# Larger groups of exact dots, the order of the last gathers and fewer address checks in a hard-max attention kernel

## The chip, the core and the metric

The kernel runs on one core of one Trainium2 chip. Its time is device microseconds of one execution; several executions are timed and their median is taken. Engine names: PE is TensorE, DVE is VectorE, ACT is ScalarE, POOL is GpSimd, SP is SyncE.

## What is computed

```python
B, Sq, Sk, D = 4, 4096, 4096, 128          # q, k, v in float32
logits = q @ k.transpose(0, 2, 1)
best = argmax(logits, axis=-1)
out = v[b, best, :]
```

For each of 16384 query rows the key with the largest dot product is found, and the value row of the same index is the result. No softmax is taken.

## The kernel before

**Tiles.** The 16384 queries are 128 tiles of 128 rows (`T = 128`), 32 tiles to a batch (`NQT = 32`). Keys come in groups of four. TensorE forms fp16 sums and differences of keys, so that the maximum of a group can be had from few products; ScalarE (`A`, `E`) and VectorE (`W`) evict them. `W` holds, for each query and each of 1024 groups, a score in the upper half of a word and the group's code in the lower half. `MAX8` (L264) takes the eight largest words of a row, so the best group comes with its score.

**Which of the four keys.** For the best group the kernel gathers one row of fp16 differences per query from a scratch copy of the keys (`k16`, 768 bytes) with an indirect DMA on GpSimd (L282, tile `kg`, "key gather" below). VectorE multiplies it with the query (`dots`: `prod` L300, `p1` L305, `p2` L308, reduction to `D` L310) and picks the largest of four (`pick`, L320 to L333). The result `win` is the index of the value row. It is gathered by an indirect DMA on GpSimd (L341, tile `vr`, "value gather" below) and stored by SP (L346).

**Chunks.** `cuts` (L682) divides the tiles into chunks: twelve of eight tiles up to tile 96, seven of four up to 124, one of two, and the last two tiles on a path of their own (`gather_whole`, `dots_whole`, `pick_whole`, in fp32). A pick treats one chunk. A dot treats `m` tiles: four where the chunk ends at tile 72 or before (`T - 56`), two after that (L776).

**The order of the work** is written out by hand: the tile framework keeps the order of the program on every engine. Iteration `it` (0 to 127) issues the products of tile `it`, the fold L260 of tile `it - 1`, the maximum L264 of tile `it - 2`, and twice a `step`, which lets the running dots, picks and flag work go on by an instruction or so. A four-tile dot yields `("wait", 1)`, one iteration, between most of its instructions; a two-tile dot goes on at the next step. Then `gathers(it - 2)` makes the candidates (L276) when a group of `m` tiles is complete and puts its key gathers into `near_q`; `issue(it)` (L743) takes from the queues what GpSimd issues in this iteration:

- from `near_q` one key gather, or two when more than `behind`'s limit are queued;
- from `fast` one gather for flagged rows, at most every second iteration;
- from `late_q` up to two value gathers, as `room` allows. `room` grows by `rate` an iteration (2.42, 2.5, 2.55, 3.0 by the iteration's number) and falls by one for each gather issued. A value tile's store follows two iterations later through SP.

GpSimd runs its gathers in this order, each one after the one before.

**The end.** Queries whose best two scores lie close together are flagged and computed again in fp32. The first 64 tiles' flags are treated inside the loop (`flag_segment`), the last 64 by `flags_last` after it: it gathers the listed queries and three candidate groups each (L512, tiles `FQ` and `FK`, "group gathers" below), computes exact dots (`exact`, L594), gathers the value rows (`FV`, L512 again) and scatters them to the output (L541). Before the group gathers it issues `LATE = 6` value gathers, after them the rest of `late_q`. Value gathers and the gathers of `flags_last` have an address check (`bounds_check`): an index beyond the table is skipped without error. Key gathers have none.

Of the kernel before, what the change touches and what calls it, by code (L numbers as in the profile page):

```python
# [17 lines left out]
IOA = bass.IndirectOffsetOnAxis  # L18
# [3 lines left out]
TAU = 8.0  # L22
NEAR = 0.5
SLOTS = 6
LATE = 6
NKG = 6


# [1 line left out]
def kernel(ctx, tc, q, k, v, out):  # L30
    nc = tc.nc
    B, Sq, D = q.shape
    Sk = k.shape[1]
    P = 128
    NQT = Sq // P
    T = B * NQT
# [229 lines left out]
    fast, near_q, late_q = [], [], []  # L266
    kg_t, cand_t = {}, {}
    done, stores, marks = set(), set(), set()
    wait_q = []

    def gather(c, t0, n):
        c0, c1 = chunks[c]
        if t0 == c0:
            cand_t[c] = sp.tile([P, c1 - c0], U32, tag=f"cand{c1 - c0}", name=f"cand_{c}", bufs=6)
        x = cand_t[c][:, t0 - c0:t0 - c0 + n]
        nc.vector.tensor_scalar(out=x, in0=TOP.bitcast(U32)[:, t0:t0 + n, 0], scalar1=IDX, scalar2=IDX,  # L276
                                op0=OP.bitwise_and, op1=OP.bitwise_xor)
        kg = rp.tile([P, 4, 3, P], FP16, tag="kg", name=f"kg_{t0}", bufs=NKG)[:, 0:n]
        assert len(kg_t) < NKG
        kg_t[t0] = kg  # L280
        for j in range(n):
            near_q.append(lambda j=j: nc.gpsimd.indirect_dma_start(  # L282
                out=kg[:, j].rearrange("p f d -> p (f d)"), out_offset=None, in_=k16[t0 // NQT],
                in_offset=IOA(ap=x[:, j:j + 1], axis=0)))
        mark = lambda: done.add(("kg", t0))
        marks.add(mark)
        near_q.append(mark)
        start(dots(c, t0, n), "dots", c)
# [24 lines left out]
    def pick(c, t0, t1):  # L313
        n = t1 - t0
        b, qt = t0 // NQT, t0 % NQT
        d = D_t[c % 4][:, 0:n, :]
        yield "until", lambda: all(("dot", x) in done for x in range(t0, t1)), 0
        cand = cand_t.pop(c)
        mx = sp.tile([P, n, 1], FP32, tag=f"mx{n}", name=f"mx_{c}")
        nc.vector.tensor_reduce(out=mx[:, :, 0], in_=d, axis=AX_X, op=OP.max)  # L320
        yield "dve",
        near = sp.tile([P, n, 4], FP32, tag=f"near{n}", name=f"near_{c}")
        nc.vector.scalar_tensor_tensor(out=near, in0=d, scalar=NEAR, in1=mx.to_broadcast([P, n, 4]),
                                       op0=OP.add, op1=OP.is_ge)
        yield "dve",
        sel = sp.tile([P, n, 4], FP32, tag=f"sel{n}", name=f"sel_{c}")
        nc.vector.tensor_tensor(out=sel, in0=near, in1=iota8.unsqueeze(1).to_broadcast([P, n, 4]), op=OP.mult)
        yield "dve",
        nc.vector.tensor_reduce(out=CNT[:, t0:t1], in_=sel, axis=AX_X, op=OP.add)
        done.add(("cnt", c))  # L330
        yield "cnt",
        win = sp.tile([P, n], U32, tag=f"win{n}", name=f"win_{c}")
        nc.vector.scalar_tensor_tensor(out=win, in0=CNT[:, t0:t1], scalar=float(b * Sk - 8), in1=cand, op0=OP.add, op1=OP.add)  # L333
        for i in range(0, n, 4):
            put_values(c, i, n, win, out[b].rearrange("(p t) d -> p t d", p=P)[:, qt + i:qt + min(i + 4, n)])

    def put_values(c, i, n, win, dst):
        vr = rp.tile([P, 4, P], FP32, tag="vr", name=f"vr_{c}_{i}", bufs=10)
        m = min(4, n - i)
        for j in range(m):  # L340
            late_q.append(lambda j=j: nc.gpsimd.indirect_dma_start(out=vr[:, j, :], out_offset=None, in_=v_flat,  # L341
                                                                   in_offset=IOA(ap=win[:, i + j:i + j + 1], axis=0),
                                                                   bounds_check=B * Sk - 1, oob_is_err=False))

        def store():
            nc.sync.dma_start(out=dst, in_=vr[:, 0:m])  # L346
            if i + m == n:
                done.add(("out", c))

        stores.add(store)  # L350
        late_q.append(store)

    def put_rec(t0, t1):
        nc.sync.dma_start(out=rec.rearrange("(p t) w -> p t w", t=T)[:, t0:t1, :], in_=TOP.bitcast(U32)[:, t0:t1, :])
# [111 lines left out]
    def flags_last(t0, t1, ready, fill, late):  # L466
# [44 lines left out]
        def get(dst, src, idx, hi):  # L511
            nc.gpsimd.indirect_dma_start(out=dst, out_offset=None, in_=src, in_offset=IOA(ap=idx, axis=0),  # L512
                                         bounds_check=hi - 1, oob_is_err=False)

        late(LATE)
        get(FK[:, 0, :], k_flat, gb[:, 0:1], B * Sk)
# [39 lines left out]
    def gather_whole(t):  # L556
        i = t - (T - 2)
        if i == 0:
            X_t["c"] = sp.tile([P, 2], U32, tag="xc", name="xc", bufs=1)
        c = X_t["c"][:, i:i + 1]  # L560
        nc.vector.tensor_scalar(out=c, in0=TOP.bitcast(U32)[:, t:t + 1, 0], scalar1=IDX, scalar2=IDX | (B - 1) * Sk,
                                op0=OP.bitwise_and, op1=OP.bitwise_xor)
        kk = X_t[i] = fp.tile([P, 512], FP32, tag=f"xk{i}", name=f"xk{i}")
        near_q.append(lambda: nc.gpsimd.indirect_dma_start(out=kk, out_offset=None, in_=k_flat, in_offset=IOA(ap=c, axis=0)))
# [114 lines left out]
    dpart(0, 1)  # L679
    nc.vector.tensor_copy(out=iota_h, in_=iota_r)  # L680
    nc.vector.tensor_copy(out=rec2[:, :, 1], in_=iota_p.to_broadcast([P, SLOTS]))
    cuts = list(range(0, T - 32 + 1, 8)) + list(range(T - 28, T - 3, 4)) + [T - 2, T]  # L682
    chunks = list(zip(cuts[:-1], cuts[1:]))
    SEGS = [0, T // 2, T]
    live = []
# [1 line left out]
    def start(g, kind, c=None):  # L687
        live.append({"g": g, "kind": kind, "c": c, "wake": 0, "until": None, "n": 0})
# [40 lines left out]
    def take_late(n):  # L729
        while n > 0 and late_q:  # L730
            g = late_q.pop(0)
            n -= g not in stores
            g()
        while late_q and late_q[0] in stores:
            wait_q.append((clock[0] + 2, late_q.pop(0)))
# [3 lines left out]
    def put_out(now):  # L739
        while wait_q and wait_q[0][0] <= now:  # L740
            wait_q.pop(0)[1]()

    def issue(it):  # L743
        n = 0
        clock[0] = it
        put_out(it)
        behind = len([g for g in near_q if g not in marks]) > (2 if it >= TAIL else 4)
        while near_q and (n < 1 + behind or near_q[0] in marks):
            g = near_q.pop(0)
            n += g not in marks  # L750
            g()
        if fast and it >= rest[0]:
            fast.pop(0)()
            rest[0] = it + 2
            n += 1
        if it < 16:
            take_late(2 if n == 0 and len(late_q) > 4 else 1)
            return
        b, qt = it // NQT, it % NQT
        busy = 0.7 if qt % 2 == 0 and (10 <= qt < 18 and b + 1 < B or 18 <= qt < 26 and b + 2 < B) else 0.0  # L760
        if qt in (13, 17) and b + 1 < B:
            busy += 1.0
        rate = 2.42 if it < 72 else 2.5 if it < 104 else 2.55 if it < 120 else 3.0
        room[0] = min(room[0] + rate - busy, 3.0) - n
        for i in range(2):
            if room[0] >= 1 and late_q:
                take_late(1)
                room[0] -= 1

    room = [0.0]  # L770

    def gathers(t):
        if t >= T - 2:
            gather_whole(t)
        for c, (t0, t1) in enumerate(chunks):
            m = 4 if t1 <= T - 56 else 2  # L776
            if t0 <= t < t1 and t < T - 2 and (t - t0) % m == m - 1:
                gather(c, t - m + 1, m)
            if t == t0 and t < T - 2:
                start(pick(c, t0, t1), "pick", c)  # L780
        if t % 8 == 7:
            put_rec(t - 7, t + 1)
        if t == SEGS[1] - 1:
            last = [c for c, x in enumerate(chunks) if x[1] == t + 1][0]
            start(flag_segment(0, t + 1, lambda: ("cnt", last) in done, lambda: ("out", last) in done), "flags")
# [6 lines left out]
    for it in range(T):  # L792
# [35 lines left out]
        if it >= 2:  # L828
            gathers(it - 2)
        issue(it)  # L830

    def flush():
# [21 lines left out]
    screen(T)  # L854
    top(T - 2)
    gathers(T - 2)
    flush()
    fold(T - 1)
    late_now(1)
    top(T - 1)  # L860
    gathers(T - 1)
    flush()
    assert not left("flags") and not fast
# [42 lines left out]
```

## Time and profile before

| | |
|---|---|
| Median of 6 runs | 531.04 us (525.3 to 534.13) |
| Profiled execution, its own time | 519.81 us |
| Its span, first to last instruction | 517.9 us |
| Mean granted TensorE clock | 0.905 |
| Value gathers (L341), `vr<-in_v_dram,win` | 126, mean 1040 ns |
| Key gathers (L282) | 126, mean 986 ns |
| Products of the dots (L300), two tiles each | 63, mean 549 ns |
| Fold (L260) and maximum (L264) | 128 each, mean 1303 and 1222 ns |
| Start of the last fold, of the last maximum | 480.30, 481.63 us |
| End of the span | 517.9 us |

The profile is of one execution, which was shorter than each of the six timed runs. Times inside it are microseconds from the span's start. Start-to-start distances can be shorter than durations, since the next instruction of an engine may start before the one before has ended. "Issue" as the reason of a wait means that the profile shows nothing the engine waited for.

### The profile page before, as it was taken

How to read it: one execution, taken by the hardware profiler on the slowest of the kernel's cores; microseconds unless marked ns; L12 is line 12 of the kernel's file. 1: busy time of each engine (PE TensorE's matmuls, PEld its weight loads, DVE VectorE, ACT ScalarE, POOL GpSimd, SP SyncE). 2: the span in 40 equal slices, each digit the busy share in tenths (PEclk: the TensorE clock that was granted, in tenths of full speed). 3: DMA queues.
4: the chain of work that ended last, by engine and by line, in shares of the span. 5: the costliest groups of instructions: out<-in, count | busy, mean ns of one | idle time of the engine just before them, and what ended most of it. 6: DMA issues, size and time to landing. Idle time of an engine off the chain costs nothing.

```text
span 517.9 us, 6303 instructions
## 1 busy us (share of the span) xinstructions
PE 401.6 (78%) x1830; PEld 172.5 (33%) x1830; DVE 411.2 (79%) x770; ACT 381.4 (74%) x437; POOL 309.1 (60%) x335
## 2 busy tenths in 40 slices
PE   8999999979859997879788873849875976978010
PEld 4444444424314442334334331313331322333000
DVE  3688999969949997679959992957995866979842
ACT  3999999969849996789778863848874965977000
POOL 9244557765745777456746774463775673654771
PEclk9999999989979999899979996987997996999555
DMA  7936895622266996222438831441223131222341
GB/s 139 209 58 110 147 125 130 110 76 80 73 132 99 157 157 128 65 72 68 114 83 145 146 91 36 88 116 51 78 72 89 44 105 46 71 73 66 83 135 38
DMA packets 52869, 50.55 MB, mean 98 GB/s; under 512 B 34136, under 2 KB 40890, under 8 KB 52832
## 3 DMA queue, kind: packets, MB, share of 16 engines
q0 software_dynamic: 19072, 33.87, 33.9%
q1 hardware_dynamic: 33760, 16.26, 13.1%
q8 instruction: 14, 0.23, 0.2%
q14 instruction: 23, 0.19, 0.1%
HBM read 40.05 MB, written 14.55 MB: 105 GB/s over the span
## 4 chain that ended last, share of the span: by engine, by line
PE 28%; issue 26%; ACT 23%; POOL 10%; DVE 6%; DMA 4%; another core or an unknown queue 2%; POOLq 0%; ACTq 0%; DVEq 0%
ACT A L234 18%; PE psn L225 9%; PE pd L225 9%; PE psn L244 9%; POOL vr L341 5%; ACT E L247 4%; POOL kg L282 4%; DMA vr<-in_v_dram,win 2%; DVE TOP L264 2%; DVE W L260 2%; DMA natk<-in_k_dram 1%; PE uk L202 1%; DMA kg<-k,cand 1%; PE uk L201 0%
## 5 line engine op out<-in xcount | busy, mean ns | idle before, releaser
L234 ACT ACTIVATE A<-pd 128x1024 f16<-128x1024 f32 x256 | 260.4, 1039 | 43.8 <-PE pd L225 21.4
L260 DVE SCALAR_TENSOR_TENSOR W<-psn,E 128x1024 int16<-128x1024 f32 x128 | 166.7, 1303 | 77.8 <-PE psn L244 36.9
L282 POOL DMA_INDIRECT kg<-k,cand x126 | 124.2, 986 | 141.7 <-DVE cand L276 107.7
L225 PE MATMUL pd<-kT,qT 128*128 128x512 f16 x512 | 158.9, 393 | 38.1 <-issue 19.7
L225 PE MATMUL psn<-kT,qT 128*128 128x512 f16 x512 | 158.7, 392 | 32.2 <-ACT A L234 13.6
L225 PEld LDWEIGHTS <-qT 128*128 128x128 f16 x1024 | 100.6, 100 | 215.0 <-issue 133.0
L341 POOL DMA_INDIRECT vr<-in_v_dram,win x126 | 131.0, 1040 | 50.0 <-issue 37.0
L244 PE MATMUL psn<-A,identh 128*128 128x512 f16 x512 | 159.0, 393 | 0.0
L264 DVE MAX8 TOP<-W 128x8 f32<-128x1024 f32 x128 | 156.4, 1222 | 0.0
L247 ACT ACTIVATE E<-psn 128x1024 int16<-128x1024 f32 x128 | 132.0, 1031 | 21.5 <-PE psn L244 14.1
L244 PEld LDWEIGHTS <-identh 128*128 128x128 f16 x512 | 51.2, 100 | 65.7 <-issue 8.5
L300 DVE TENSOR_TENSOR prod<-kg,natq 128x768 f16<-128x768 f16 x63 | 34.6, 549 | 2.4 <-DMA kg<-k,cand 1.5
L205 ACT ACTIVATE kT<-uk 128x256 f16<-128x256 f32 x48 | 19.8, 413 | 22.5 <-remote 13.9
L201 PE MATMUL uk<-identh,natk 128*128 128x128 f16 x96 | 15.8, 218 | 6.0 <-ACT E L247 5.7
L305 DVE TENSOR_TENSOR p<-prod 128x384 f16<-128x384 f16 (+1 forms) x45 | 19.3, 430 | 0.1
L310 DVE TENSOR_REDUCE D<-p 128x6 f32<-128x192 f16 (+1 forms) x45 | 18.7, 418 | 0.1
L202 PEld LDWEIGHTS <-natk 128*128 128x128 f16 x96 | 9.3, 97 | 13.4 <-issue 10.8
L308 DVE TENSOR_TENSOR p<-p 128x192 f16<-128x192 f16 (+1 forms) x45 | 13.0, 290 | 0.1
L66 POOL DMA_DIRECT2D natk<-in_k_dram x19 | 11.3, 601 | 0.8 <-POOLq L890 0.8
L201 PEld LDWEIGHTS <-natk 128*128 128x128 f16 x96 | 9.4, 98 | 5.6
L484 PE MATMUL fp_e<-n_e,tri 128*128 128x1 f32 x2 | 0.6, 362 | 13.2 <-DVE e_e L478 13.2
L69 POOL DMA_DIRECT2D natq<-in_q_dram x15 | 9.1, 611 | 0.0
(152 smaller groups left out, 141.9 us busy)
## 6 DMA issues: line engine op xcount, KB each, us to landing
out_dram<-vr SPq DMA_DIRECT2D x31, 256.0 KB
natq<-in_q_dram POOLq DMA_DIRECT2D x12, 256.0 KB
natk<-in_k_dram POOLq DMA_DIRECT2D x10, 256.0 KB
k<-kd SPq DMA_DIRECT2D x18, 128.0 KB
k<-natk POOLq DMA_DIRECT2D x6, 384.0 KB
kg<-k,cand POOLq DMA_INDIRECT x126
vr<-in_v_dram,win POOLq DMA_INDIRECT x126
natk<-in_k_dram POOLq DMA_DIRECT2D x8, 128.0 KB
```

Source lines behind the costliest of these rows:

```text
L201: nc.tensor.matmul(out=o, lhsT=natk[b % 2][:, h, 4 * m + x, :], rhs=identh, start=True, stop=False)
L205: nc.scalar.activation(out=kT[b % 2][:, c:c + 256], in_=ps, func=AF.Copy)
L225: nc.tensor.matmul(out=ps[:, n * 512:(n + 1) * 512], lhsT=qT[b % 2][:, qt * P:(qt + 1) * P], rhs=kT[b % 2][:, u * 1024 + n * 512:u * 1024 ...
L234: nc.scalar.activation(out=A, in_=ps, func=AF.Abs)
L244: nc.tensor.matmul(out=ps[:, n * 512:(n + 1) * 512], lhsT=identh, rhs=A[:, n * 512:(n + 1) * 512], start=False, stop=True)
L247: nc.scalar.activation(out=E, in_=ps, func=AF.Relu, scale=QSCALE)
L260: nc.vector.scalar_tensor_tensor(out=W_t[t % NW].bitcast(I16)[:, 1::2], in0=ps, scalar=QSCALE, in1=E, op0=OP.mult, op1=OP.max)
L264: nc.vector.max(out=TOP[:, t, :], in_=W_t[t % NW].bitcast(FP32))
L282: near_q.append(lambda j=j: nc.gpsimd.indirect_dma_start(out=kg[:, j].rearrange("p f d -> p (f d)"), out_offset=None, in_=k16[t0 // NQT], ...
L300: nc.vector.tensor_tensor(out=prod[:, i:i + h], in0=kg[:, i:i + h], in1=natq[b % 2][:, x + i - b * NQT:x + i + h - b * NQT, :].unsqueeze(2 ...
L305: nc.vector.tensor_tensor(out=p1, in0=prod[:, :, :, 0:64], in1=prod[:, :, :, 64:128], op=OP.add)
L341: late_q.append(lambda j=j: nc.gpsimd.indirect_dma_start(out=vr[:, j, :], out_offset=None, in_=v_flat, in_offset=IOA(ap=win[:, i + j:i + j ...
```

## The change

Five edits:

1. Dots of four tiles up to tile 108 in place of 72. Tiles 72 to 107 then have nine dots of four tiles in place of 18 of two.
2. Value gathers have the address check only in chunks that end after tile 96, the last batch; the 96 gathers before that have none.
3. In the last iteration (`it >= T - 1`) all queued key gathers are issued and no value gather.
4. `rate` is 2.5 up to iteration 100 and 2.42 after it, in place of 2.5 up to 104, 2.55 up to 120 and 3.0 at the end.
5. `LATE` is 4 in place of 6: four value gathers go before the group gathers of `flags_last`.

The new text of `cuts` gives the same cuts as before.

```diff
-LATE = 6
+LATE = 4
...
         m = min(4, n - i)
+        edge = dict(bounds_check=B * Sk - 1, oob_is_err=False) if chunks[c][1] > T - NQT else {}
         for j in range(m):
             late_q.append(lambda j=j: nc.gpsimd.indirect_dma_start(out=vr[:, j, :], out_offset=None, in_=v_flat,
-                                                                   in_offset=IOA(ap=win[:, i + j:i + j + 1], axis=0),
-                                                                   bounds_check=B * Sk - 1, oob_is_err=False))
+                                                                   in_offset=IOA(ap=win[:, i + j:i + j + 1], axis=0), **edge))
...
-    cuts = list(range(0, T - 32 + 1, 8)) + list(range(T - 28, T - 3, 4)) + [T - 2, T]
+    cuts = list(range(0, 96 + 1, 8)) + list(range(96 + 4, T - 3, 4)) + [T - 2, T]
...
-        while near_q and (n < 1 + behind or near_q[0] in marks):
+        while near_q and (n < 1 + behind or near_q[0] in marks or it >= T - 1):
...
-        rate = 2.42 if it < 72 else 2.5 if it < 104 else 2.55 if it < 120 else 3.0
+        rate = 2.42 if it < 72 else 2.5 if it < 100 else 2.42
         room[0] = min(room[0] + rate - busy, 3.0) - n
         for i in range(2):
-            if room[0] >= 1 and late_q:
+            if room[0] >= 1 and late_q and it < T - 1:
...
-            m = 4 if t1 <= T - 56 else 2
+            m = 4 if t1 <= 108 else 2
```

## The prediction

> **What bounds the kernel now.** I read the page's busy shares first.
>
> ```profile
> PE 401.6 (78%) x1830; PEld 172.5 (33%) x1830; DVE 411.2 (79%) x770; ACT 381.4 (74%) x437; POOL 309.1 (60%) x335
> ```
>
> No engine is busy all the time, so the shares are an average over stages. The busy time in stretches of 25 us separates them (columns: PE, weight loads, VectorE, ScalarE, GpSimd, granted TensorE clock, DMA share, GB/s).
>
> ```profile
> 275.00:300.00 25.00, 21.47 (x106) 9.28 (x104) 24.45 (x63) 21.71 (x26) 16.45 (x17) 1.00 0.77 135
> ...
> 425.00:450.00 25.00, 19.18 (x70) 7.44 (x70) 18.14 (x35) 17.64 (x19) 11.76 (x12) 0.80 0.22 60
> ```
>
> The reader is to see two kinds of stretch. In the first VectorE is busy for 24.45 of 25 us at a granted clock of 1.00: VectorE sets the pace. In the second the clock is 0.80 and nobody is full. The starts of the 128 folds (L260) in VectorE's timeline show where such time lies: 14 of the 127 steps between folds take 5.2 to 10.8 us, 104 us together, the others about 3 us. With 14 x 3 = 42 us taken off, 62 us are lost there, in nine spells of about 7 us. Tiles 72 to 107, which the change treats, hold six of these long steps (73, 86, 87, 93, 104, 105); the other 30 steps are full of VectorE work.
>
> Then the waits (who waited for whom: us in total, times, longest):
>
> ```profile
> POOL kg L282 <- DVE cand L276: 107.7, 28, 13.8
> ...
> DVE prod L300 <- DMA kg<-k,cand: 1.5, 2, 1.0
> ```
>
> GpSimd waits for VectorE's candidates, 107.7 us; VectorE waits for a gathered key row 1.5 us in all. So a shorter gather on GpSimd is worth nothing in the loop.
>
> **Four-tile dots for tiles 72 to 107.** Groups of VectorE by line and shape (count | busy us, mean ns of one):
>
> ```profile
> L305 DVE TENSOR_TENSOR p<-prod 128x768 f16<-128x768 f16 x18 | 9.9, 551 | 0.0
> L310 DVE TENSOR_REDUCE D<-p 128x12 f32<-128x384 f16 x18 | 9.7, 537 | 0.0
> L305 DVE TENSOR_TENSOR p<-prod 128x384 f16<-128x384 f16 x27 | 9.4, 349 | 0.1
> L310 DVE TENSOR_REDUCE D<-p 128x6 f32<-128x192 f16 x27 | 9.2, 339 | 0.1
> L308 DVE TENSOR_TENSOR p<-p 128x192 f16<-128x192 f16 x27 | 6.7, 250 | 0.1
> L308 DVE TENSOR_TENSOR p<-p 128x384 f16<-128x384 f16 x18 | 6.3, 350 | 0.0
> L276 DVE TENSOR_SCALAR cand<-TOP 128x2 uint32<-128x2 uint32 x27 | 4.8, 178 | 0.0
> ...
> L276 DVE TENSOR_SCALAR cand<-TOP 128x4 uint32<-128x4 uint32 x18 | 3.0, 166 | 0.1
> ```
>
> Of four tiles, two dots of two tiles cost 2 x (349 + 339 + 250 + 178) = 2232 ns, beside four tiles' worth of products (L300, two instructions either way). One dot of four costs 551 + 537 + 350 + 166 = 1604 ns. That is 628 ns less for each of nine groups of four: 5.65 us, the upper bound, since neighbours overlap. From start to start in VectorE's timeline the second operations take less than their durations: a two-tile dot's sum, second sum, reduction and candidate advance it by 0.26 + 0.16 + 0.25 + 0.08 us, a four-tile one's by 0.47 + 0.26 + 0.45 + 0.08 us; 1.50 - 1.26 = 0.24 us a group, 2.2 us for nine, the lower bound. Between them lies a row that holds all effects: eight undisturbed tiles with four-tile dots (folds 64 to 72, 228.87 to 252.25) take 23.38 us, 11.69 for four; four undisturbed tiles with two-tile dots (folds 115 to 119, 438.15 to 450.53) 12.38. The second have picks of four tiles in place of eight; a pick's five instructions advance VectorE by about 0.08 us each, 0.40 a chunk, so 0.20 of the 0.69 us is theirs. 0.49 us are left for the dots, 4.4 us for nine groups, and I take this one. In the spells TensorE is late and VectorE idle, so I count 30 of 36 tiles: 3.7 us (bounds 1.9 to 5.65).
>
> Next behind VectorE is ScalarE: its three evictions start 0.92 us apart, 2.77 us a tile, and on every other tile up to 95 a key unit (413 ns) is added, 2.98 us a tile. VectorE needs fold and maximum 1.20 + 1.14, half a product of 0.46, a quarter of 1.26 and of 0.20 for picks, 2.94 us, and the first half's flag work (L363 to L607, some 10 us of short instructions in tiles 73 to 102) adds 0.3. So ScalarE takes over only where no flag work stands, and takes back 0.04 us on some tiles, inside the bounds. The candidates come after the fourth tile in place of the second, so a group's four key gathers follow each other and the dot begins later; no edge is lost: below tile 72, where dots are of four already, the wait for a gathered row is part of the same 1.5 us. If that cover went, each of nine groups could show the 2.9 us from a gather's start to its landing (483.20 to 486.16 below), less what VectorE does meanwhile.
>
> **The address check.** An undisturbed value gather with a check has a median of 1002 ns (L341), a key gather without 959 ns (L282); 43 ns for 96 gathers, and a 29 ns move each, are 4 to 7 us of GpSimd. It is hidden by the 107.7 us above: 0 on the path. Were GpSimd the bound, the gain would be these 4 to 7 us.
>
> The gathers meet another cost. Value gathers that start while VectorE multiplies fp16 rows take 1.21 us (106.22 beside a product from 106.00) or 1.30 us (411.51 beside one from 411.39) in place of 1.00. Four-tile sums are longer single instructions (551 ns) though fewer; I take 0. The Trainium skill, "SBUF — State Buffer", section "SBUF: two separate sides", speaks against the change here: descriptors of a GpSimd-issued DMA cannot be written while VectorE holds the shared port pair in a two-port mode. By that rule nine sums that are longer by 0.20 us would hold GpSimd 1.8 us more; here the rows show only the 0.2 to 0.3 us, and no run shows the port.
>
> **The pace of value gathers and the end.** Following `room`, `near_q` and `late_q` through the iterations: before, the queue of value gathers runs empty several times after iteration 114, and 118 of 128 are issued when the loop ends; after, with 2.42 in place of 2.55 and 3.0, and nothing taken at iteration 127, 115. For the end GpSimd's and then VectorE's timeline:
>
> ```profile
> 479.33 0.94 POOL L282 DMA_INDIRECT kg<-k,cand  x1 [4.73 <-DVE cand L276]
> ...
> 483.20 1.28 POOL L282 DMA_INDIRECT kg<-k,cand  x1 [0.30 <-issue]
> ...
> 496.52 0.99 POOL L512 DMA_INDIRECT FK<-in_k_dram,gb_e  x1 [0.30 <-issue]
> ...
> 504.33 1.00 POOL L341 DMA_INDIRECT vr<-in_v_dram,win_w  x1 [0.30 <-issue]
> 510.84 1.00 POOL L512 DMA_INDIRECT FV<-in_v_dram,xw_fe  x1 [5.51 <-DVE xw_fe L607]
> ```
>
> ```profile
> 486.16 0.56 DVE L300 TENSOR_TENSOR prod<-kg,natq 128x768 f16<-128x768 f16 x1 [0.98 <-DMA kg<-k,cand]
> ```
>
> Before: key row 124, two value gathers, key row 125 at 483.20; VectorE waits 0.98 us for it at 486.16. After: both key rows first, so 125 starts at 480.58, lands 2.9 us later at 483.5, and the dot starts when its forerunner is done, at 485.18. Everything down to the row numbers (L505 at 493.78, done 493.93, L509 done 494.85) comes 0.98 us earlier. GpSimd after: key rows 479.33 and 480.58, whole row at 481.84, value gather 483.1, whole row 484.4, and LATE = 4 value gathers 485.7 to 490.9. The first group gather (L512) starts then not at 496.52 but when L505 has given its index: 493.2, 3.3 us earlier, and the fourth at 497.1. But three value gathers stood behind them before, and now 6 + 2 = 8: at 1.30 us from start to start the last starts at 497.1 + 8 x 1.30 = 507.5 (before 504.33). From that start to the point where GpSimd is free for FV (L512, last) the chain of waits shows 504.33 to 507.55, 3.2 us: free at 510.7. FV's index comes from VectorE at 510.45 - 0.98 = 509.5, and 0.4 us later could FV start: 509.9. So GpSimd is last, and FV starts at 510.7 against 510.84. The end keeps its place: -0.1 us, between -1.0 (GpSimd's wrap-up is shorter) and +1.0 (the 0.98 us is not won). Group gathers come 3.3 us earlier and pay nothing, since VectorE reaches them (L594) only after its own work at 504.69. LATE and the order move GpSimd's queue and, through it, SP's stores: the last store now begins near 511.5, takes the about 2 us of before, and ends before the last scatter, which lands near 516.
>
> **Sum.** 3.7 + 0.1 = 3.8 us off the profiled execution's own 519.81 us (span 517.9), 516.0 us. That execution was 2.1% below the median of the runs shown, 531.04; by the ratio 0.9927 the median becomes 527.2 us. The unknown costs alone give -6.7 to -0.9 us, 524 to 530.
>
> **Rivals.** Fewer spells: if the spells of lost clock belong to times at which TensorE waits for VectorE, a shorter VectorE step drops one of the four in the stretch, about 7 us; with the 3.8 us, 520 us. For it: the clock is 1.00 up to 108 us, where steps are even and short, and the last 54 tiles, with longer steps, have long gaps oftener. Against: steps of 2.8 to 3.0 us precede the gaps at folds 31, 40 and 63 too. The granted clock of 0.80 in 425 to 450 us follows the 9.4 us step from 419.44. The Trainium skill, "TensorE: Matmul & The Clock Gate", Part 1, says that TensorE falls to half rate after an idle window of about 3.4 us; by it a denser TensorE has fewer spells, and the sum would be this rival's.
>
> More spells (slower): if the spells answer to how densely TensorE works, the denser middle earns one more. A mean one costs 7 us, 531.04 + 7 - 3.8 = 534.2; a long one as at folds 86 and 87 (17.3 us in place of 6) 538.5, two mean ones 541. For it: none in the first 108 us, and the median of runs is itself 11 us over this execution, as much as one or two. Against: a denser TensorE does not lose more. From fold 32 to 74 (149 us) 26 us go beyond 42 steps of 2.93 us, 17%; from 74 to 127 (216 us) 41 us beyond 53 steps of 3.3 us, 19%. It is slower by over 1% from one long spell.
>
> Nothing: ScalarE or the spells take all that VectorE saves; 530 to 532 us.
>
> **Numbers.** The forecast (524 to 530) has 0.40, fewer spells, or full durations with a smaller share of such time, 0.32, nothing 0.11, more spells 0.17. A measurement of this kernel, whose runs lie between 525.3 and 534.13, can tell about 1% from no change: 525.7 and 536.4. Of the forecast 0.08 lies below 525.7, so faster is 0.32 + 0.08 = 0.40; of the last case 0.15 lie above 536.4; 0.45 are left within 1%. The range from 519.5 to 536 leaves out the far parts of the two spell cases, about 0.05 below and 0.15 above.
>
> **What would show it.** 18 four-tile dots become 27, 27 of two tiles become 9; VectorE's busy time falls by 5 to 6 us, the undisturbed steps of 72 to 107 by 0.12 us a tile. Value gathers of the first 96 tiles take about 0.96 us. Two key rows stand side by side at the end, the dot behind them waits for nothing, eight value gathers follow the group gathers, and from the last maximum to FV the time stays at 29.2 us (481.63 to 510.84). It is wrong if VectorE's products wait for gathers for more than 3 us in all, if FV starts over 1 us later after the last maximum, or if long steps are more or fewer than 14.

## The result, and the profile after

| | before | after |
|---|---|---|
| Median, all runs | 528.44 us (517.78 to 542.34, 46 runs) | 519.32 us (510.36 to 531.97, 20 runs) |
| Ratio, 95% interval | | 0.9865 (0.9815 to 0.9915) |
| Profiled execution, its own time | 519.81 us | 523.9 us |
| Its span, mean granted clock | 517.9 us, 0.905 | 522.0 us, 0.901 |
| Folds 72 to 108 (start to start) | 154.82 us | 149.15 us |
| Of it, beyond 3 us in steps over 5 us | 31.3 us | 25.5 us |
| Last maximum's start to the end of the span | 36.2 us | 37.6 us |

The kernel is 1.35% faster; the forecast was 0.7%. A ratio is taken over the runs within 1.5% of each kernel's fastest (6 of 20 and 14 of 46 here), so it need not be the ratio of two medians, and where the runs of a kernel spread over 20 us it leans against the kernel with fewer runs. By the medians of all runs the kernel is 1.7% faster. The two profiled executions must not be set against each other by their lengths: before's was among the shortest of its runs, after's is 4.6 us above its own median. What can be compared in them is the parts.

The first view is the page of after: the busy shares, and the rows of VectorE and of the granted clock in 40 slices.

```profile
PE 403.9 (77%) x1830; PEld 173.5 (33%) x1830; DVE 410.7 (79%) x734; ACT 381.2 (73%) x437; POOL 303.8 (58%) x335
...
DVE  3689999979859996774989988586992867989860
...
PEclk9999999989969999897989999888996896999555
```

VectorE has 36 instructions fewer (734 for 770), but only 0.5 us less busy time, and VectorE's slices still drop from 9 to between 8 and 2 inside the loop, the clock's to between 8 and 6: the stretches of low clock are still there. The next view gives VectorE's groups of after by line and shape (count | busy us, mean ns of one).

```profile
L305 DVE TENSOR_TENSOR p<-prod 128x768 f16<-128x768 f16 x27 | 15.0, 554 | 0.0
L310 DVE TENSOR_REDUCE D<-p 128x12 f32<-128x384 f16 x27 | 14.6, 542 | 0.0
L308 DVE TENSOR_TENSOR p<-p 128x384 f16<-128x384 f16 x27 | 9.5, 352 | 0.0
...
L276 DVE TENSOR_SCALAR cand<-TOP 128x4 uint32<-128x4 uint32 x27 | 4.6, 169 | 0.1
...
L305 DVE TENSOR_TENSOR p<-prod 128x384 f16<-128x384 f16 x9 | 3.2, 351 | 0.1
```

There are 27 dots of four tiles and nine of two. The waits say that the later candidates cost nothing: VectorE's products waited for no gathered row (2.4 us idle before them in before), and GpSimd still waits for VectorE:

```profile
POOL kg L282 <- DVE cand L276: 97.8, 24, 14.2
```

```profile
L300 DVE TENSOR_TENSOR prod<-kg,natq 128x768 f16<-128x768 f16 x63 | 34.7, 553 | 0.0
...
L342 POOL DMA_INDIRECT vr<-in_v_dram,win x126 | 126.2, 1002 | 65.1 <-issue 36.2
```

(The second of these fences is from the page's costliest groups. L342 is before's L341, one line lower.) A value gather has gone from a mean of 1040 to 1002 ns; the 96 without a check have a median of 945 ns.

The end is where the profile does not do what was forecast. GpSimd's timeline of after, the last 25 us; before's was shown with the prediction, and one more line of it stands below:

```profile
497.25 1.06 POOL L512 DMA_INDIRECT FK<-in_k_dram,gb_e  x1 [3.49 <-DVE row_e L509]
...
501.21 1.00 POOL L512 DMA_INDIRECT FK<-in_k_dram,gb_e  x1 [0.30 <-issue]
...
511.77 1.00 POOL L342 DMA_INDIRECT vr<-in_v_dram,win_w  x1 [0.30 <-issue]
513.08 0.99 POOL L512 DMA_INDIRECT FV<-in_v_dram,xw_fe  x1 [0.31 <-issue]
517.79 1.02 POOL L541 DMA_INDIRECT out_dram<-FV,rowk_e  x1 [3.72 <-DMA out_dram<-vr]
```

```profile
513.67 1.02 POOL L541 DMA_INDIRECT out_dram<-FV,rowk_e  x1 [1.83 <-DMA FV<-in_v_dram,xw_fe]
```

In before the scatter waited for its own rows (`FV`), 1.83 us. In after it waits 3.72 us for `out_dram<-vr`, a store of ordinary value rows. The chain of waits of after shows that store's way (start us, us, what):

```profile
511.77 2.69 DMA vr<-in_v_dram,win_w
514.47 0.46 SPq L346
514.93 0.06 issue
514.99 1.81 DMA out_dram<-vr
```

The last value gather starts at 511.77, lands 2.69 us later, SP takes it up, the store lands at 516.80, and 0.99 us later the scatter starts. The scatter may not write its rows before the ordinary rows are in place. So the end of this execution is set by the last value gather, 6.0 us ahead of the scatter. Counted from the last maximum (484.39 in after, 481.63 in before), the last value gather starts at 27.4 in place of 22.7 us, `FV` at 28.7 in place of 29.2, and the scatter at 33.4 in place of 32.0. VectorE had the row numbers for `FV` ready 22.3 us after the last maximum in after, 28.8 us in before: in after `FV` stood behind value gathers alone, for 6.4 us.

### The profile page after: what moved, and what is told of

Read it like the earlier page. It is cut to its first block, busy times and chain, and to the rows that moved or that the text cites. A ratio compares the mean times of both kernels' runs of the same rounds, so it can differ in the third digit from the quotient of the medians.

```text
span 522.0 us, 6163 instructions
## 1 busy us (share of the span) xinstructions
PE 403.9 (77%) x1830; PEld 173.5 (33%) x1830; DVE 410.7 (79%) x734; ACT 381.2 (73%) x437; POOL 303.8 (58%) x335
## 4 chain that ended last, share of the span: by engine, by line
PE 36%; ACT 28%; issue 18%; DVE 9%; another core or an unknown queue 4%; DMA 3%; POOL 1%; POOLq 1%; ACTq 0%; SPq 0%; DVEq 0%
ACT A L234 21%; PE psn L225 12%; PE pd L225 11%; PE psn L244 11%; ACT E L247 6%; DVE TOP L264 3%; DVE W L260 3%; DMA natk<-in_k_dram 1%; POOL vr L342 1%; DVE prod L300 1%; PE uk L201 1%; DMA FK<-in_k_dram,gb_e 1%; DMA vr<-in_v_dram,win_w 1%; PE uk L202 0%
## 5 line engine op out<-in xcount | busy, mean ns | idle before, releaser
L234 ACT ACTIVATE A<-pd 128x1024 f16<-128x1024 f32 x256 | 261.0, 1040 | 53.2 <-PE pd L225 25.3
L225 PE MATMUL pd<-kT,qT 128*128 128x512 f16 x512 | 160.1, 396 | 37.9 <-ACT A L234 20.4
L342 POOL DMA_INDIRECT vr<-in_v_dram,win x126 | 126.2, 1002 | 65.1 <-issue 36.2
L300 DVE TENSOR_TENSOR prod<-kg,natq 128x768 f16<-128x768 f16 x63 | 34.7, 553 | 0.0
L305 DVE TENSOR_TENSOR p<-prod 128x768 f16<-128x768 f16 (+1 forms) x36 | 18.1, 503 | 0.1
L310 DVE TENSOR_REDUCE D<-p 128x12 f32<-128x384 f16 (+1 forms) x36 | 17.7, 491 | 0.1
L308 DVE TENSOR_TENSOR p<-p 128x384 f16<-128x384 f16 (+1 forms) x36 | 11.8, 327 | 0.1
```

What stands on the lines that cost most here:

```text
L225: nc.tensor.matmul(out=ps[:, n * 512:(n + 1) * 512], lhsT=qT[b % 2][:, qt * P:(qt + 1) * P], rhs=kT[b % 2][:, u * 1024 + n * 512:u * 1024 ...
L234: nc.scalar.activation(out=A, in_=ps, func=AF.Abs)
L300: nc.vector.tensor_tensor(out=prod[:, i:i + h], in0=kg[:, i:i + h], in1=natq[b % 2][:, x + i - b * NQT:x + i + h - b * NQT, :].unsqueeze(2 ...
L305: nc.vector.tensor_tensor(out=p1, in0=prod[:, :, :, 0:64], in1=prod[:, :, :, 64:128], op=OP.add)
```

## The experiments

The theory behind the prediction was: VectorE sets the pace outside the spells of low clock, so the dots save about 4 us; the check is hidden; the end keeps its place. Its rivals were fewer spells, more spells, and nothing. The first three kernels each made one part of the change alone; the fourth took away four-tile dots everywhere, for the opposite direction.

**Dots alone** (before, with the one line changed).

```diff
-            m = 4 if t1 <= T - 56 else 2
+            m = 4 if t1 <= 108 else 2
```

> Before with edit 1 alone (four-tile dots up to tile 108). Theory A (VectorE's own savings, as forecast): 0.7% faster than before (-3.7 us), undisturbed VectorE work of folds 72 to 107 shorter by 2 to 5.6 us, the end as before (last maximum to end of span 36 us). Theory B (a shorter VectorE step also loses less time to spells of low clock): 1.2 to 1.5% faster, nearly all of the change's gain. Theory C (the gain comes from GpSimd's lighter gathers or from the end): within 0.4% of before.

**Address check alone** (before; no check on the value gathers of chunks up to tile 96).

```diff
+        edge = dict(bounds_check=B * Sk - 1, oob_is_err=False) if chunks[c][1] > T - NQT else {}
...
-                                                                   in_offset=IOA(ap=win[:, i + j:i + j + 1], axis=0),
-                                                                   bounds_check=B * Sk - 1, oob_is_err=False))
+                                                                   in_offset=IOA(ap=win[:, i + j:i + j + 1], axis=0), **edge))
```

> Before with edit 2 alone (no address check on the first 96 value gathers). GpSimd is 4 to 6 us less busy, value gathers of the first 96 tiles have a median near 0.945 us in place of 1.005. Theories A and B: 0 +- 0.4%, since GpSimd waits for VectorE. Theory C: 0.6 to 1.0% faster.

**The end alone** (before, with edits 3, 4 and 5: the key gathers of the last iteration, `rate`, `LATE`).

```diff
-LATE = 6
+LATE = 4
...
-        while near_q and (n < 1 + behind or near_q[0] in marks):
+        while near_q and (n < 1 + behind or near_q[0] in marks or it >= T - 1):
...
-        rate = 2.42 if it < 72 else 2.5 if it < 104 else 2.55 if it < 120 else 3.0
+        rate = 2.42 if it < 72 else 2.5 if it < 100 else 2.42
...
-            if room[0] >= 1 and late_q:
+            if room[0] >= 1 and late_q and it < T - 1:
```

> Before with edits 3, 4 and 5 alone (key gathers first in the last iteration, the lower rate, LATE 4). By the queues 9 value gathers are left at the end in place of 7, 7 of them behind the group gathers in place of 3. The profile of the changed kernel has the last scatter 33.4 us after the last maximum in place of 32.0, since it waits for the last value store. Theory D (the end is longer): last maximum to end of span 37 to 38 us in place of 36.2, time +0.2%. The forecast's step: 36.1 us, time 0. Theory C: 0.5% faster or more.

**Two-tile dots everywhere** (before).

```diff
-            m = 4 if t1 <= T - 56 else 2
+            m = 2
```

> Before with dots of two tiles everywhere (18 four-tile dots of the first 72 tiles become 36 of two): edit 1 turned round and doubled. Theory A: 18 x 0.49 = 8.8 us more VectorE work, of which some 85% shows: 1.4% slower. Theory B: about twice that, 2.5 to 3% slower. Theory C: within 0.4%.

All four on one chip, beside before at 528.46 us (513.82 to 540.33, 24 runs):

| | median us | runs | ratio (95%) | ratio of the medians of all runs | last maximum to end of span, us |
|---|---|---|---|---|---|
| dots alone | 530.08 | 6 | 1.0174 (1.0073 to 1.0276) | 1.003 | 36.5 |
| check alone | 528.19 | 12 | 1.0024 (0.9845 to 1.0203) | 0.999 | 36.4 |
| end alone | 527.71 | 6 | 1.0110 (1.0016 to 1.0204) | 0.999 | 35.2 |
| two-tile dots | 521.85 | 12 | 0.9963 (0.9899 to 1.0027) | 0.987 | 40.6 |

No part alone gains. The two columns of ratios differ because the first takes three of the six runs of dots alone, and five of six of end alone, beside the five shortest of before's 24; the slowdowns of 1 to 2% in it are not in the medians. Most striking is the last row: two-tile dots make VectorE do more (busy 415.1 us, 842 instructions) and were expected to be 1.4% slower, yet all twelve of its runs lie below before's median: by the medians the opposite of edit 1 came out 1.3% faster, nearly as much as the change itself. (Its last scatter starts 32.6 us after the last maximum, 32.0 in before; the long end lies behind that scatter, in this one execution.) With runs of one kernel 26 us apart, parts worth 1 to 5 us cannot be read here. The end alone has an end of 35.2 us, shorter than before's 36.2, where 37 to 38 was expected for the theory that the end is longer. What varies is the spells: in these profiles the steps over 5 us between folds lose 55.6, 58.2, 68.0 and 58.4 us beyond 3 us each.

**A chip without spells.** The next four kernels went to another chip together, and before took 444.65 us there (443.58 to 445.54, 19 runs), 84 us less, with all runs within 2 us. The four are: the whole change; the change with `LATE` back at 6; before with added work on VectorE (an unused 128x256 `memset` after each fold); and before with added work on TensorE (one 256-column matmul per tile, whose result is overwritten). The added work leaves the output as it is.

> The changed kernel again, beside the kernel before on one chip: the size of the effect. First comparison: -1.35% (0.9815 to 0.9915). Its parts alone showed nothing clear (dots alone 530.1, checks alone 528.2, end alone 527.7 us against 528.5). Theory A or B: 519 to 524 us, the parts add up. Theory E (TensorE's clock sets the time to fold 108, 389 to 398 us in all profiles so far whatever VectorE does, so a schedule's gain is small and not the sum of saved instructions): within 1% of before, 523 to 529 us.

```diff
-LATE = 4
+LATE = 6
```

> The changed kernel with LATE 6 in place of 4. In the changed kernel's profile GpSimd idles 3.5 us ahead of the group gathers (8.37 + 1.00 to 12.86 us after the last maximum) and the last scatter (33.40) waits for the last value store. Two value gathers moved into that hole: the last value gather starts 2.6 us earlier after the last maximum (24.8 in place of 27.4), last maximum to end of span 35.0 to 35.5 us in place of 37.6, time 0.4 to 0.5% below the changed kernel's in this call. If the scatter waits for something else, no change of the end.

```diff
             fold(it - 1)
+            nc.vector.memset(wz, 0.0)
```

> Before with one more memset of an unused constant (128x512 fp16, 272 ns in the profile of before) on VectorE after each fold, 127 x 0.2 to 0.27 us = 25 to 34 us more VectorE work. Theory A (VectorE sets the pace outside the spells): +20 to +28 us, 4 to 5% slower. Theory E (TensorE's clock sets it): under +8 us, since the spells give back what VectorE takes.

```diff
         ps = pp.tile([P, 1024], FP32, tag="u", name=f"pd_{t}_{x}")
+        if x == 0:
+            b, qt = t // NQT, t % NQT
+            nc.tensor.matmul(out=ps[:, 0:256], lhsT=qT[b % 2][:, qt * P:(qt + 1) * P],
+                             rhs=kT[b % 2][:, 1024:1280], start=True, stop=True)
```

> Before with one more matmul of 256 columns per tile, whose result the next matmul overwrites: 1/24 more TensorE work (0.108 us a tile at full clock, TensorE then at some 2.8 us a tile, under VectorE's 2.92). Theory A: 0 to +1%. Theory E: the spells come with TensorE's work, 1/24 of the 370 us behind the first spell is +15 us, 2.5 to 3.5% slower, with as long undisturbed steps and more time in long steps.

| | median us | ratio (95%) |
|---|---|---|
| the change | 443.25 | 0.9970 (0.9960 to 0.9981) |
| the change, `LATE = 6` | 440.89 | 0.9919 (0.9905 to 0.9932) |
| added work on VectorE | 509.49 | 1.1465 (1.1450 to 1.1480) |
| added work on TensorE | 445.24 | 1.0020 (1.0008 to 1.0031) |

First, who sets the pace. One matmul of 256 columns more per tile (128 more in all, and 8.4 us more of PE's busy time than in the change) costs 0.2%; a `memset` of 0.27 us per tile costs 14.65%, three times the 4 to 5% expected. The page of the changed kernel on this chip, its VectorE and clock rows:

```profile
PE 378.9 (86%) x1830; PEld 167.9 (38%) x1830; DVE 406.2 (92%) x734; ACT 375.8 (85%) x437; POOL 306.1 (69%) x335
...
DVE  2688999999999999999999999999999999999830
...
PEclk9999999999999999999999999999999999997555
```

VectorE is at 9 from the fifth slice to the end of the loop, and there is not one step over 5 us. Its busy time in stretches (the columns of the prediction's second view) says the same:

```profile
253.00:278.00 25.00, 22.57 (x115) 10.02 (x114) 24.93 (x46) 22.81 (x28) 18.56 (x19) 1.00 0.61 124
...
303.00:328.00 25.00, 21.72 (x93) 8.85 (x92) 24.93 (x61) 22.68 (x25) 18.07 (x19) 1.00 0.32 90
```

Second, the dots. Starts of fold 72, fold 108 and the last maximum in VectorE's timeline: with the change, then with the dots as before. For the latter the kernel with the added matmul stands in, whose order on VectorE and GpSimd is before's and whose time is within 0.2% of it (its line numbers are four higher than before's).

```profile
228.13 1.29 DVE L260 SCALAR_TENSOR_TENSOR W<-psn,E 128x1024 int16<-128x1024 f32 x1
...
342.80 1.29 DVE L260 SCALAR_TENSOR_TENSOR W<-psn,E 128x1024 int16<-128x1024 f32 x1
...
405.47 1.23 DVE L264 MAX8 TOP<-W 128x8 f32<-128x1024 f32 x1
```

```profile
228.57 1.31 DVE L264 SCALAR_TENSOR_TENSOR W<-psn,E 128x1024 int16<-128x1024 f32 x1
...
348.13 1.30 DVE L264 SCALAR_TENSOR_TENSOR W<-psn,E 128x1024 int16<-128x1024 f32 x1
...
410.61 1.23 DVE L268 MAX8 TOP<-W 128x8 f32<-128x1024 f32 x1
```

Fold 72 to fold 108 takes 342.80 - 228.13 = 114.67 us with four-tile dots and 348.13 - 228.57 = 119.56 with two: 4.9 us less. The added matmul makes the stand-in slower than before by 0.6 us (medians) to 0.9 us (ratio 1.0020); were all of that in this stretch, 4.0 us would be left, so the edits' share there lies between 4.0 and 4.9 us. (The dots alone were not run without spells; the change in this stretch also has edit 2 and, from tile 100 on, edit 4.) At the last maximum the change is 5.14 us ahead.

What these microseconds are, the busy time from fold 72 to the last fold shows (columns as above): the change, then the stand-in, then after and before with spells.

```profile
228.13:404.14 176.01, 156.46 (x704) 66.01 (x702) 175.52 (x338) 157.34 (x174) 131.65 (x133) 1.00 0.45 106
...
228.57:409.29 180.72, 161.10 (x764) 71.97 (x761) 177.61 (x374) 159.41 (x175) 134.88 (x134) 1.00 0.44 105
...
260.42:483.06 222.64, 171.26 (x708) 69.47 (x706) 178.12 (x337) 160.46 (x175) 129.77 (x133) 0.92 0.36 83
...
252.25:480.30 228.05, 173.29 (x709) 69.86 (x707) 179.52 (x373) 161.92 (x175) 134.15 (x134) 0.90 0.35 84
```

Without spells the stretch is 4.7 us shorter. VectorE's own work is 2.1 us of that (177.61 to 175.52). The other 2.6 us are time in which VectorE stood idle in the stand-in (3.1 us) and not in the change (0.5 us); nearly all of it is products that wait for gathered key rows:

```profile
DVE prod L304 <- DMA kg<-k,cand: 3.8, 7, 1.1
```

Six of these seven waits, 2.8 us, lie in the stretch; in the change there is none. Half of that lies behind fold 108, and tiles from 108 on have dots of two in both kernels, so it is not shown which of the edits removed these waits. With spells VectorE's own work there falls by 1.4 us (179.52 to 178.12); in dots alone it is 178.43 and 178.35 us, in check alone and end alone 179.2 to 180.1.

Third, the end takes almost all of that back. GpSimd's timeline of the change on this chip, then of the stand-in:

```profile
417.14 1.05 POOL L512 DMA_INDIRECT FK<-in_k_dram,gb_e  x1 [2.29 <-DVE row_e L509]
...
431.78 0.99 POOL L342 DMA_INDIRECT vr<-in_v_dram,win_w  x1 [0.30 <-issue]
433.08 0.99 POOL L512 DMA_INDIRECT FV<-in_v_dram,xw_fe  x1 [0.30 <-issue]
438.42 1.02 POOL L541 DMA_INDIRECT out_dram<-FV,rowk_e  x1 [4.36 <-DMA out_dram<-vr]
```

```profile
433.45 1.00 POOL L345 DMA_INDIRECT vr<-in_v_dram,win_w  x1 [0.30 <-issue]
435.48 0.99 POOL L516 DMA_INDIRECT FV<-in_v_dram,xw_fe  x1 [1.03 <-DVE xw_fe L611]
438.89 1.02 POOL L545 DMA_INDIRECT out_dram<-FV,rowk_e  x1 [2.42 <-DMA FV<-in_v_dram,xw_fe]
```

From the last maximum, the last value gather starts at 431.78 - 405.47 = 26.31 us in place of 433.45 - 410.61 = 22.84, `FV` at 27.61 in place of 24.87, the scatter at 32.95 in place of 28.28. The end is 4.7 us longer. Of that 2.7 us arise because `FV` waits behind eight value gathers in place of three, 1.9 us because the scatter then waits for the last store. (The profiled execution of the change was the longest of its eight, 1.3 us above their median.) The reader should look at the first line's bracket too: GpSimd stands idle for 2.29 us before the first group gather, with `LATE = 4` value gathers used up and eight more in its queue.

With `LATE = 6` this pause is filled:

```profile
417.49 1.06 POOL L512 DMA_INDIRECT FK<-in_k_dram,gb_e  x1 [0.30 <-DVE XD L569]
...
429.27 1.00 POOL L342 DMA_INDIRECT vr<-in_v_dram,win_w  x1 [0.30 <-issue]
430.57 0.99 POOL L512 DMA_INDIRECT FV<-in_v_dram,xw_fe  x1 [0.30 <-issue]
434.81 1.02 POOL L541 DMA_INDIRECT out_dram<-FV,rowk_e  x1 [3.25 <-DMA out_dram<-vr]
```

The last value gather is 2.2 us earlier after the last maximum (405.20 here), the scatter 3.3 us, and the median falls by 2.36 us. So edit 5 costs about 0.5% where it can be measured, and the change without it is the better one there.

**Parts again, on a third chip, with spells** (before 538.02 us, 532.32 to 545.29, 11 runs): the three parts with their edits as above, and the change with `LATE = 6` and a faster pace of value gathers from iteration 100 on. What is expected below for a chip without spells stays untested, since this chip had them.

> Four-tile dots alone once more, since the first comparison lay on a chip with a throttled clock (runs of one kernel 514 to 541 us) and told nothing. On a chip without spells: folds 72 to 108 take 114.6 us as in the changed kernel, 4.9 less than in the kernel before (119.6 with the extra matmul), the end stays at 32.5 us: 1.0 to 1.2% faster, more than the whole change (0.3%). On a throttled chip the median is within 1.5% of before and says nothing; folds 72 to 108 are then read without their long steps.

> Edits 3, 4 and 5 alone once more. On a chip without spells: the loop as before, last maximum to end of span some 35 to 36 us in place of 32.5, since seven value gathers stand behind the group gathers and the scatter waits for the last store: 0.6 to 0.9% slower. The forecast's step had 0.

> Edit 2 alone once more. On a chip without spells: value gathers of tiles 0 to 95 take a median of 0.945 us in place of 1.00, GpSimd 4 to 5 us less busy, folds and the end as before: 0 +- 0.2%. If GpSimd is next to VectorE on the path somewhere: up to 1% faster.

```diff
-LATE = 4
+LATE = 6
...
-        rate = 2.42 if it < 72 else 2.5 if it < 100 else 2.42
+        rate = 2.42 if it < 72 else 2.5 if it < 100 else 3.0
```

> The changed kernel with LATE 6 and rate 3.0 in place of 2.42 from iteration 100 on: by the queues one value gather fewer is left at the end, five behind the group gathers in place of six. Beside LATE 6 alone (0.8% faster than before, end 33.8 us) the last value gather starts 1.3 us earlier: end 32.5 us, 1.1% faster than before. If the rate slows the loop by crowding GpSimd, folds 108 to 127 take longer than 61.3 us.

| | median us | ratio (95%) | ratio of the medians of all runs | folds 72 to 108, us | lost beyond 3 us in long steps there / elsewhere, us | last maximum to end of span, us |
|---|---|---|---|---|---|---|
| dots alone | 536.71 | 0.9947 (0.9876 to 1.0017) | 0.998 | 151.78 | 25.1 / 51.8 | 37.2 |
| end alone | 541.92 | 1.0063 (0.9999 to 1.0126) | 1.007 | 162.32 | 39.9 / 37.9 | 34.7 |
| check alone | 541.85 | 1.0088 (1.0039 to 1.0137) | 1.007 | 158.04 | 34.2 / 47.9 | 36.9 |
| the change, `LATE = 6`, `rate` 3.0 | 528.07 | 0.9837 (0.9779 to 0.9896) | 0.982 | 143.88 | 20.1 / 41.8 | 34.0 |

By the medians of all runs dots alone is within 0.3% of before on both chips; the two intervals do not meet, but the first of them rests on three runs beside five. End alone and check alone do not gain; why check alone should be 0.9% slower here, where 0 was expected, is open. Read without their long steps, folds 72 to 108 have a mean step of 3.58 us with dots alone, 3.54 with end alone and 3.55 with check alone. The last kernel is 1.6% faster; its interval overlaps the change's own, 0.9815 to 0.9915, which was measured beside other runs of before. The two versions were not run side by side with spells; without them `LATE = 6` was.

## Why the prediction was right or wrong

**VectorE sets the pace outside the spells: right.** From fold 72 to the last fold VectorE is busy for 175.52 of 176.01 us in the change without spells, and more work on TensorE cost 0.2%. The kernel with more work on VectorE points the same way (1.1465), but it lost nearly twice what was added (64.8 us for 34.5), so it says more of the rhythm of the engines than of VectorE alone. More work on ScalarE, next in the prediction's order and busy for 85%, was not tried.

**The dots, 0.49 us a group, 4.4 us for nine: right in the sum, half of it for another reason.** Without spells the stretch behind fold 72 became 4.7 us shorter, but VectorE's own work there by 2.1 us only, 0.23 us a group. That is the prediction's start-to-start sum, its lower bound of 2.2 us. The row between the bounds, from which 0.49 us was taken, asked for twice as much, and what filled the gap is a term that the prediction put at nothing: waits for gathered key rows, 2.8 us in the stand-in and none in the change. That the two add up to the forecast is luck. VectorE's busy time was forecast to fall by 5 to 6 us, which is the sum of durations. That sum did fall (L305, L308, L310 and L276: 59.0 to 53.7 us), but busy time counts overlapping neighbours once, and fell by 0.5 us with spells and 2.2 us without (408.4 in the stand-in, 406.2 in the change). The undisturbed steps of tiles 72 to 107 were to be 0.12 us shorter; without spells all 36 steps are by 0.14 us in the mean (3.32 to 3.19), with spells the 30 steps under 5 us have a mean of 3.52 us in both profiles.

**The candidates' later gathers hidden: right.** Products waited 0.0 us for gathered rows in the profile of after, and none waited in the loop with dots alone.

**The address check hidden, 0: right as far as it can be seen.** A value gather went from 1.00 to 0.945 us, GpSimd's busy time from 309.1 to 303.8 us, inside the 4 to 7 us named. The kernels with this part alone show no gain: 1.0024 with a wide interval, and 1.0088. The 1.8 us more of GpSimd time that the prediction worked out for the longer sums did not show: with dots alone GpSimd was busy for 307.7 and 307.3 us, in before for 309.1.

**The end, -0.1 us: this is the step that failed.** The queue itself was followed correctly: eight value gathers did come to stand behind the group gathers, the last forecast at 25.9 us after the last maximum and measured at 26.3 without spells and 27.4 with them. But two things in that step were wrong.

First, "the last store … ends before the last scatter, which lands near 516". The store was compared with the scatter's landing. What counts is the scatter's start: it waits until the stores have landed. By the forecast's own numbers the store ends at 511.5 + 2 = 513.5, and the scatter starts 1.0 us later (516.80 to 517.79 in after), at 514.5; before's started at 513.67. That alone is +0.8 us; from `FV` to the scatter the profiles show 1.9 us more, in both places.

Second, `FV` was put at 510.7 against 510.84, "between -1.0 and +1.0". That reading rested on before's profiled execution, in which `FV` waited 5.51 us for VectorE's row numbers. On the chip without spells the same order waited 1.03 us, since VectorE's end work was done 24.5 us after the last maximum in place of 28.8. There the room for five more value gathers did not exist, and `FV` came 2.7 us later, past the 1 us that the prediction had named as a sign of being wrong. In the profile of after `FV` started 28.7 us after the last maximum, 0.5 us earlier than in before: with spells the time held, but not its reason. VectorE's row numbers were to come 0.98 us earlier and came 6.5 us earlier (22.3 in place of 28.8 us), and the eight value gathers in front of `FV` used that up.

So the end cost +1.4 us in the one pair of executions and +4.7 us in the other, for -0.1 forecast. The first of these is not firm: with spells the end alone has ends of 35.2 and 34.7 us, shorter than the 36.2 to 37.2 of before, dots alone and check alone. It left seven value gathers behind the group gathers; joined with four-tile dots the same edits left eight.

**The sum, -3.8 us, 0.7%.** Without spells the ratio is 0.9970, -1.4 us by the medians; by the profiles of the change and the stand-in it is -5.1 us up to the last maximum and +4.7 behind it. With spells it is 0.9865, some 7 us of 528, and 9 us by the medians. Of that the profiles explain little: from fold 72 on VectorE's own work is 1.4 us less and the idle time before products 1.4 us less (in before's loop 0.5 us for a row and 0.9 us for nothing that the profile shows), the end 1.4 us longer. That the total came out near the forecast is luck too.

**The spells: open.** The other 6 to 8 us are left for the spells, which would be in part the first rival, "fewer spells". It is not shown. The number of long steps did not change (14 and 14), their loss was 62.0 and 55.3 us; yet after's profiled span is 4.1 us longer than before's, and up to fold 72, where the two kernels differ in the check alone, it took 8.2 us longer (260.42 and 252.25). The stretch from fold 72 to 108 speaks for the rival: the four profiled executions with four-tile dots there lost 17.4, 20.1, 25.1 and 25.5 us in long steps (dots alone on two chips, the change and its last version), the six with two-tile dots 26.0 (two-tile dots everywhere), 29.8, 31.3, 34.2, 35.0 and 39.9. But over the whole execution the two groups overlap (55.3 to 76.9 and 58.2 to 82.1), and two-tile dots everywhere has the lowest median of its comparison. Each of these is one execution of a kernel whose runs spread over 8 to 27 us.

One thing can be read of how a spell begins. In the profile of before the granted clock falls to 0.5 nine times inside the loop. Three of the stretches of 3.41 us ahead of a fall, and behind the first the stretch that follows it:

```profile
109.08:112.49 3.41, 0.83 (x4) 0.31 (x4) 1.39 (x2) 1.41 (x2) 2.80 (x3) 1.00 0.48 144
112.49:115.90 3.41, 3.41 (x10) 1.21 (x9) 0.46 (x1) 2.35 (x3) 1.27 (x2) 0.50 0.18 48
...
255.85:259.26 3.41, 0.90 (x5) 0.33 (x4) 3.06 (x7) 0.38 (x1) 2.80 (x4) 1.00 0.81 163
...
310.47:313.88 3.41, 0.38 (x4) 0.26 (x4) 0.00 (x0) 1.48 (x2) 2.50 (x3) 1.00 0.21 58
```

Ahead of every one of the nine falls the clock is 1.00 and TensorE is busy for only 0.38 to 1.59 of 3.41 us; in the one from 255.85 us VectorE is still at work. So by these records the stall of TensorE comes first and the lower clock after it: the clock is not what starts a spell. What stalls TensorE there, and which property of the order moves it, was not found. The Trainium skill, "TensorE: Matmul & The Clock Gate", section "HAM oscillation — how this bites in real kernels", has TensorE keep clear of idle gaps beyond about 3.4 us. Here shorter gaps went with a fall: in seven of the nine the longest gap of TensorE in the 8 us ahead is 1.5 to 2.7 us (the ends of matmuls are modelled), at the first fall this one:

```profile
112.25 0.81 PE L225 MATMUL psn<-kT,qT 128*128 128x512 f16 x2 [1.54 <-issue]
```

**The rivals "more spells" and "nothing"** are out for the change as a whole with spells by its interval, which ends at 0.9915. Without spells the change is 0.3% faster, close to "nothing".

## What to carry to other kernels

When work is moved behind something at the end of a kernel, follow each moved transfer to the instruction that must wait for its landing, and compare with that instruction's start, not its end. A wait of several microseconds in one execution (here 5.51 us before `FV`) is no room to spend until a second chip shows it too. When runs of one kernel differ by more than an edit is worth, measure the edit where they do not, and take steps between fixed marks rather than totals. And split such a stretch into the engine's own work and its idle time before the gain is put down to either.

## What the runs showed of the hardware

- One kernel took 444.65 us on one chip and 528.46 and 538.02 us on two others. The profiles of its variants differ by the spells: none on the first, 55 to 82 us lost in steps over 5 us on the others, with a mean granted clock of 0.957 to 0.968 against 0.88 to 0.915.
- A `memset` of 0.27 us per tile, 34.5 us in all, made the kernel 64.8 us longer. VectorE itself then stood idle for 40.2 us before the folds (7.4 us in the change on the same chip); 26.4 us of it are waits for TensorE's `psn`. That TensorE is late in turn because VectorE frees its buffers later is argued from the order of the work and was not tried by itself. The groups of VectorE by line for that kernel:

```profile
L260 DVE SCALAR_TENSOR_TENSOR W<-psn,E 128x1024 int16<-128x1024 f32 x128 | 166.8, 1303 | 40.2 <-PE psn L244 26.4 <-ACT A L234 8.9 <-ACT E L247 3.6
...
L818 DVE MEMSET wz<- 128x256 uint32 x127 | 34.5, 272 | 0.0
```

- VectorE's end work was done 24.4 and 24.5 us after the last maximum in before's order without spells (the two kernels with added work), 28.5 to 29.5 us in the six profiles of that order with spells; the clock granted to TensorE falls to 0.5 at the end in both cases. In before it waited 0.4 to 1.0 us five times on its own earlier instructions, and 1.83 and 2.16 us for what the profile calls remote. With edits 3 to 5 and `LATE = 4` the difference is not there: 21.5 us without spells, 21.1 to 22.3 with them. The cause is open.
